# A two-layer diffusion backbone in fp32: the first FFN's down product whole, by seven block products, and the late modulation in three places

## The chip, the core and the metric

The kernel runs on one core of a Trainium2 chip. Its engines run side by side, each through a queue of its own in order: TensorE (PE in the profile, PEld for its weight loads), VectorE (DVE), ScalarE (ACT), GpSimd (POOL) and SyncE (SP), which here only issues DMA transfers. TensorE writes to PSUM, 8 banks of 128 x 512 fp32 values; DVE and ACT carry sums from there to SBUF. The metric is the device time in microseconds, as the median of several runs.

## What is computed

There are 512 latent and 256 context tokens of width 1024, which are 6 tiles of 128 tokens: tiles 0 to 3 latent, 4 and 5 context. Two layers follow each other. Layer 0 has a mixer of gated linear attention and softmax attention, layer 1 a gated recurrence (HGRN2); each is followed by a SwiGLU FFN with 2816 hidden units. Every sub-layer is wrapped in norms and in a modulation that depends on the condition:

```python
m_lat = jnp.split((sc @ mod_w[l] + mod_b[l])[:, None, :], 6, axis=-1)
m_ctx = jnp.split((scc @ mod_w[l] + mod_b[l])[None, None, :], 6, axis=-1)
...
h_lat = _modulate(_rms(x_lat, norm_pre_ffn[l]), m_lat[3], m_lat[4])
x_lat = x_lat + m_lat[5] * _rms(_swiglu(h_lat, ffn_w_gate[l], ffn_w_up[l], ffn_w_down[l]), norm_post_ffn[l])
...
def _swiglu(h, w_gate, w_up, w_down):
    return (jax.nn.silu(h @ w_gate) * (h @ w_up)) @ w_down
```

The context takes the same path with `m_ctx` in layer 0; in layer 1 only latent tokens go through the FFN. So the first FFN has 6 tiles, the second 4. Each `mod_w[l]` is a 1024 x 6144 matrix that is multiplied by two vectors.

## The kernel before

**Precision.** A product in fp32 is made from three matmuls. Each operand is split into a rounded part H (an ACT cast) and a rest L (a DVE subtraction), and `mm3` (line 686) adds H.H, H.L and L.H. So each block of weights costs a DMA of fp32 values into a `raw` tile, a cast on ACT and a subtraction on DVE (`unit`, line 671). The pool `wp` holds three `raw` buffers and four each of `wH` and `wL`.

**Seven products.** `seven` (line 775) multiplies two blocks of 128 hidden columns (a pair) by all tokens by a scheme of the Strassen-Winograd kind. The weights are cut into 2 x 2 blocks, and so are the activations (`Forms`, line 63: halves of the width by halves of the tokens, n = 384 tokens in the first FFN and 256 in the second). Seven products of 4 x 3 matmuls stand for eight. `pair_operands` (line 737) makes the weights' sums and splits on DVE and ACT. Results are put together by DVE and ACT from the banks A, B, D and E; the fourth product (U2) adds onto the bank of the first (A) after that one was copied out.

**First FFN** (`ffn`, line 1510). For each of 11 pairs it runs the gate product, then the part of the down product for the pair before, then the up product. `acc_part` (line 817) is that down part: for each of 6 tiles and two halves of the width 2 blocks by three matmuls of 512 columns, and a DVE addition into `y`. The last call takes two pairs at once and ends one tile after another: `end` runs the post-norm, the residual sum and the next layer's pre-norm on ACT, DVE and POOL (`post_pre`, line 1467), and leaves a function in `turns` that transposes the tile on PE and applies the modulation. `turn(left)` (line 1481) calls these until `left` remain. The values of the second mixer (`odd_values`, line 1308; 512 of 1024 columns) follow in between, with two of their four weight pairs held in tiles of the FFN's own pool. The first pair is special (`first`): its products start while the last tiles of the mixer's output are still being normed, and `turn` is called after 12 and after 36 of its matmuls.

**Second FFN** (`ffn_whole`, line 1613, and `down`, line 1688). All gate and up products come first; the gated activations stay in SBUF (`G`). Then the down product is made whole by seven block products: 2 x 2 blocks over tokens, hidden blocks (even and odd) and output columns. Each of the seven runs over 11 hidden blocks in 7 groups, for the 2 tiles of a token half. `operands` splits weights and activations per group, three groups ahead; sums of weight blocks are made in two SBUF tiles, the first by a DVE addition, later ones by GpSimd transfers that add in memory.

**Modulation.** `mod_vec` (line 515) computes late jobs on DVE: per 128 rows of `mod_w` a load of 0.5 MB and one multiply-add per stream and row block (line 537), then four matmuls that sum over partitions. It is a generator; each step is drawn where the FFN calls `fill`. Five jobs run so in the first FFN. `mod_group` (line 491) is the other way, on PE: 4 matmuls of 256 columns per 128 rows.

**Order.** A planner orders the instructions of each engine when the kernel is built, by their place in the program and by modelled times; where `pinned` is set, PE keeps the written order. In `ffn` it is not set, in `down` and in the second mixer's heads it is.

Of the kernel before, what the change touches and what calls it, by code (L numbers as in the profile page):

```python
# [8 lines left out]
F32 = mybir.dt.float32  # L9
# [8 lines left out]
P = 128  # L18
# [298 lines left out]
class Net:  # L317
# [196 lines left out]

    def mod_vec(self, pool, jobs, own=None, bufs=2, sums=2):
# [259 lines left out]
    def seven(self, W, h, X, fill, then=None, turned=False):  # L775
# [3 lines left out]
        c11, c12, c21, c22 = (X[:, i, n * k : n * k + n] for i in range(2) for k in range(2))  # L779
# [36 lines left out]

    def acc_part(self, parts, n, tiles, groups, ys, first, end):


        nc = self.nc  # L820

        def add(y, pt):
            if first:
                nc.scalar.copy(y, pt)
            else:
                nc.vector.tensor_tensor(y, y, pt, op=ALU.add)  # L826

        for group in groups:
            pts = {}
            for i in group:  # L830

                self.whole = not self.whole
                pt = self.mm_tile("acc") if self.whole else None
                pts[i] = pt, [pt[:, :512], pt[:, 512:]] if self.whole else [self.sc_tile("acc", x) for x in range(2)]
            for p, (units, act) in enumerate(parts):
                done = p == len(parts) - 1
                for i in group:
                    whole, halves = pts[i]
                    t = tiles[i]
                    H, L = (x[:, :, i * P % n : i * P % n + P] for x in act[i * P // n])  # L840
                    for hf in range(2):
                        cs = slice(hf * 512, hf * 512 + 512)
                        for c, unit in enumerate(units):
                            self.mm3(
                                halves[hf],
                                (H[:, c, :], L[:, c, :]),
                                (unit[0][:, 0, cs], unit[1][:, 0, cs]),
                                p == 0 and c == 0,
                                done and c == len(units) - 1,
                            )  # L850
                        if done and hf == 0:
                            self.turn(1)
                        if done and whole is None:
                            add(ys[:, t, cs], halves[hf])
                    if done:
                        if whole is not None:
                            add(ys[:, t, :], whole)
                        end(ys[:, t, :], t)
# [449 lines left out]
    def odd_values(self, fi, h, c0, tiles, us=None):  # L1308

        us = us or self.wide_units(3 * D + c0)  # L1310
        for t0 in tiles:
            pt = self.mm_tile("nat").rearrange("p (a b) -> p a b", a=2)
            for a in range(2):
                self.wide_tile(pt[:, a, :], us, h, t0 + a)
            self.nc.scalar.copy(fi[:, t0 : t0 + 2, c0 : c0 + 512], pt)
# [194 lines left out]
    def ffn(self, l, xp, yp, fp, pp, rp, h, ending, extra=None):  # L1510
# [3 lines left out]
        wg, wu, wd = I["ffn_w_gate"][l], I["ffn_w_up"][l], I["ffn_w_down"][l]  # L1514
        tiles, n = h.order, h.n
        extra = extra(fp) if extra else iter(())
        fill = lambda *_: next(extra, None)
        singles = [(i,) for i in range(len(tiles))]

        gp = rp if l else fp  # L1520
        self.banks(True)

        def gu(x):
            return fp.tile([P, 2, 2 * n], F32, tag=x, bufs=2 if x == "go" else 1, name=x)

        def gated(pool, k, g, u, HL=None, mult=True):

            g, u = (x[:, :, n * k : n * k + n] for x in (g, u))
            if mult:
                nc.vector.tensor_tensor(u, u, g, op=ALU.mult)  # L1530
            H, L = HL or h.gated_tiles(pool, k)
            nc.scalar.copy(H, u)
            nc.vector.tensor_tensor(L, u, H.bitcast(F32), op=ALU.subtract)
            return H, L

        def first():

            cur = h.gated if l else [h.gated_tiles(gp, k) for k in range(2)]
            g, u = gu("go"), gu("uo")
            us = [[self.unit_cols(w, i * P) for w in (wg, wu)] for i in range(2)]  # L1540
            h.open(xp)
            for half in range(2):
                pm = self.mm_tile("pearly")
                pts = [[self.sc_tile("pearly", x)[:, :n] for x in range(2)], [pm[:, 512 * x : 512 * x + n] for x in range(2)]]
                tok = slice(n * half, n * half + n)
                for ks in ((range(4), range(4, 8)) if half == 0 else (range(8),)):
                    for i in range(2):
                        for m in range(2):
                            for k in ks:
                                self.mm3(pts[i][m], tuple(x[:, k, :] for x in us[i][m]), h.raw(k, half), k == 0, k == KD - 1)  # L1550
                            if ks[0] == 0 and half == 0 and m == 0:
                                self.turn(1 - i)
                for i in range(2):
                    nc.scalar.activation(g[:, i, tok], pts[i][0], AF.Silu)
                    nc.vector.tensor_tensor(u[:, i, tok], g[:, i, tok], pts[i][1], op=ALU.mult)
                gated(gp, half, g, u, cur[half], False)
                if half == 0:
                    pp.release()
                    tp = self.open_pool(f"t{l}")
                    h.sums(tp)  # L1560
            h.late()
            return tp, cur

        def units(c0):
            return [self.rows_unit(wd, c0 + i) for i in range(2)]

        def product(w, c0, x, then=None):
            x = gu(x)
            self.seven(self.pair_operands(tp, w, c0 * P, [tp] if l else [], 1 + l), h, x, fill if c0 > 2 else lambda: None, then)
            return x  # L1570

        tp, cur = first()
        y = None
        todo = None
        for c0 in range(2, NFC, 2):
            g = product(wg, c0, "go", todo)
            for k in range(2):
                x = g[:, :, n * k : n * k + n]
                nc.scalar.activation(x, x, AF.Silu)
            if c0 + 2 < NFC:  # L1580
                if y is None:
                    y = yp.tile([P, len(tiles), D], F32, tag="y", bufs=1, name=f"y{l}")
# [4 lines left out]
                def todo(g=g, u=u, cur=cur):  # L1587
                    for k in range(2):
                        gated(gp, k, g, u, cur[k], True)
# [531 lines left out]
```

## Time and profile before

| | us |
|---|---|
| median of 3 runs | 1721.51 (1720.88 to 1721.73) |
| profiled execution | 1719.44 |
| its span, first to last instruction | 1717.5 |
| granted clock of TensorE, mean | 0.997 |

The profile is of one execution. Busy times are per engine. A row of the stretches gives the stretch, then for PE, PEld, DVE, ACT and POOL the busy time and the number of instructions, then the granted PE clock (1.00 is full), the busy share of the DMA engines and GB/s. A row of a group gives line, engine, operation, output <- inputs, shape and count, then busy time and the mean of one instruction in ns, then idle time ahead of it and what ended it. A row of waits gives who waited for whom, the sum in us, how often, and the longest. A row of the chain gives start, length and what ran.

| stretch (us) | what runs |
|---|---|
| 416 to 471 | first FFN: first pair, last tiles of the mixer's output, first pair of `seven` |
| 471 to 909 | pairs: gate, part of down, up |
| 909 to 947 | last down part with the tiles' norms |
| 947 to 1014 | values of the second mixer |
| 1361 to 1592 | second FFN, gate and up |
| 1592 to 1717 | second FFN, down product and ending |

### The profile page before, as it was taken

To read this page: it belongs to the slowest core of one execution; us is meant where nothing else is said; L and a number is where in the kernel's file an instruction comes from. 1 tells how busy PE (TensorE), PEld (TensorE's weight loads), DVE (VectorE), ACT (ScalarE), POOL (GpSimd) and SP (SyncE) were. 2 spreads that over 40 slices of the span, in tenths; PEclk is the share of its full clock that TensorE was granted. 3 is DMA by queue.
4 is the path that set the end of the run, shared out by engine and by line. 5 is a ranking of instruction groups with operands and counts; after the bars stand their busy time and mean duration, and the time that the engine had idled before them with its cause. 6 is when DMAs were issued, how large, how long until landed. Compare 5 with 4: busy or idle time off the path is not lost.

```text
span 1717.5 us, 32485 instructions
## 1 busy us (share of the span) xinstructions
PE 1665.1 (97%) x13446; PEld 1494.9 (87%) x13446; DVE 1301.8 (76%) x2110; ACT 894.8 (52%) x1552; POOL 96.8 (6%) x114
## 2 busy tenths in 40 slices
PE   6999998999999999999999999999999999999997
PEld 5899987887999988999998888988888899999776
DVE  4889678835968999797667418788774599987977
ACT  4745568846453233333346526666564565554554
POOL 1004110000000000000001000000000100000220
PEclk9999999999999999999999999999999999999999
DMA  9641012144334456362224322111124334332883
GB/s 323 191 150 39 2 51 88 49 160 144 102 94 123 151 172 195 109 212 74 74 74 171 106 66 63 51 51 51 50 65 145 123 111 123 100 114 76 224 187 105
DMA packets 177343, 195.87 MB, mean 114 GB/s; under 512 B 6918, under 2 KB 141612, under 8 KB 177196
## 3 DMA queue, kind: packets, MB, share of 16 engines
q1 hardware_dynamic: 170704, 181.56, 33.9%
q0 software_dynamic: 4560, 8.65, 2.8%
q10 hardware_dynamic: 1932, 3.59, 0.6%
q8 instruction: 105, 1.72, 0.4%
q14 instruction: 42, 0.34, 0.1%
HBM read 184.31 MB, written 9.46 MB: 113 GB/s over the span
## 4 chain that ended last, share of the span: by engine, by line
PE 77%; DVE 11%; DMA 5%; ACT 4%; issue 2%; POOL 1%; ACTq 0%; DVEq 0%; POOLq 0%; SPq 0%
PE nat L355 12%; PE a L355 10%; PE acc L355 8%; PE ff L355 8%; PE E L355 7%; PE oproj L355 5%; PE b L355 3%; PE D L355 3%; PE fq L355 3%; PE x L355 2%; PE gqk L355 2%; DMA mraw<-in_mod_w_dram 2%; DVE macc L537 2%; PE o L355 2%; PE S L355 1%
## 5 line engine op out<-in xcount | busy, mean ns | idle before, releaser
L355 PE MATMUL nat<-wH,x 128*128 128x256 f32 (+2 forms) x944 | 215.7, 318 | 3.0 <-ACT x L648 2.6
L734 ACT CAST wH<-raw 128x1024 fp32r<-128x1024 f32 x120 | 125.0, 1051 | 176.6 <-DVE y L826 42.6
L680 DVE TENSOR_TENSOR wL<-raw,wH 128x1024 fp32r<-128x1024 f32 (+1 forms) x104 | 124.1, 1202 | 83.0 <-ACT wH L679 82.2
L355 PEld LDWEIGHTS nat<-wH,x 128*128 128x128 f32 x944 | 157.6, 190 | 18.5 <-ACT x L648 3.6
L735 DVE TENSOR_TENSOR wL<-raw,wH 128x1024 fp32r<-128x1024 f32 x120 | 145.5, 1219 | 34.1 <-ACT wH L734 34.1
L679 ACT CAST wH<-raw 128x1024 fp32r<-128x1024 f32 (+1 forms) x104 | 106.8, 1038 | 80.3 <-PE nat L355 23.7
L355 PE MATMUL nat<-wL,x 128*128 128x256 f32 (+2 forms) x472 | 148.5, 315 | 0.0
L607 POOL TENSOR_TENSOR rs<-ms,neghalf 128x1 f32<-128x1 f32 (+2 forms) x62 | 58.1, 939 | 1277.7 <-DVE ms L605 1277.6
L537 DVE SCALAR_TENSOR_TENSOR macc<-mraw,scT,macc 128x1024 f32<-128x1024 f32 x98 | 122.7, 1277 | 7.3 <-DMA mraw<-in_mod_w_dram 6.9
L355 PE MATMUL ff<-x,wH 128*128 128x512 f32 (+1 forms) x512 | 127.6, 340 | 0.0
L355 PE MATMUL acc<-wH,gH 128*128 128x512 f32 x264 | 104.5, 396 | 1.9 <-DVE y L826 1.3
L355 PE MATMUL acc<-wL,gH 128*128 128x512 f32 x264 | 103.2, 391 | 1.4 <-DVE wL L680 1.4
L355 PE MATMUL acc<-wH,gL 128*128 128x512 f32 x264 | 103.2, 391 | 0.0
L355 PE MATMUL oproj<-wH,x 128*128 128x512 f32 x320 | 101.9, 395 | 0.6 <-ACT x L1241 0.6
L355 PEld LDWEIGHTS ff<-x,wH 128*128 128x128 f32 x512 | 87.3, 190 | 10.1
L355 PEld LDWEIGHTS nat<-wL,x 128*128 128x128 f32 x472 | 89.8, 190 | 5.2
L929 ACT COPY qkh<-arr 128x512 f32<-128x512 f32 x112 | 70.0, 641 | 36.3 <-DVE arr L934 32.1
L355 PE MATMUL ff<-x,wL 128*128 128x256 f32 (+1 forms) x256 | 86.2, 337 | 0.0
L826 DVE TENSOR_TENSOR y<-y,acc 128x512 f32<-128x512 f32 (+1 forms) x81 | 68.9, 861 | 22.6 <-PE acc L355 21.2
L759 DVE TENSOR_TENSOR raw<-raw 128x512 f32<-128x512 f32 x120 | 82.4, 687 | 2.0
L934 DVE TENSOR_TENSOR arr<-arr,f 128x512 f32<-128x512 f32 x112 | 74.1, 686 | 1.9 <-ACT qkh L929 0.3
L355 PE MATMUL a<-T,wH 128*128 128x384 f32 (+1 forms) x320 | 70.4, 309 | 1.7 <-ACT G L797 1.7
(417 smaller groups left out, 4401.4 us busy)
## 6 DMA issues: line engine op xcount, KB each, us to landing
mraw<-in_mod_w_dram SPq DMA_DIRECT2D x80, 512.0 KB, 4.0
raw<-in_ffn_w_gate_dram SPq DMA_DIRECT2D x44, 512.0 KB, 3.9
raw<-in_ffn_w_up_dram SPq DMA_DIRECT2D x44, 512.0 KB, 4.4
raw<-in_odd_w_in_dram SPq DMA_DIRECT2D x40, 512.0 KB, 3.8
raw<-in_ffn_w_down_dram SPq DMA_DIRECT2D x24, 512.0 KB, 3.6
mraw<-in_mod_w_dram SPq DMA_DIRECT2D x32, 256.0 KB, 6.1
raw<-in_even_w_in_dram SPq DMA_DIRECT2D x16, 512.0 KB, 3.9
x<-xr SPq DMA_DIRECT2D x14, 512.0 KB, 2.6
```

The lines of the kernel that those rows point to most:

```text
L355: return self.pin(self.nc.tensor.matmul(*a, **k))
L537: nc.vector.scalar_tensor_tensor(a, u, w, a, op0=ALU.mult, op1=ALU.add)
L607: nc.gpsimd.tensor_tensor(rs, ms, self.neghalf.to_broadcast([P, w]), op=ALU.pow)
L679: nc.scalar.copy(H[:, :m], raw[:, :m])
L680: nc.vector.tensor_tensor(L[:, :m], raw[:, :m], H[:, :m].bitcast(F32), op=ALU.subtract)
L734: self.nc.scalar.copy(H, f)
L735: self.nc.vector.tensor_tensor(L, f, H.bitcast(F32), op=ALU.subtract)
L759: add = lambda o, x, y: nc.vector.tensor_tensor(o, x, y, op=ALU.add)
L826: nc.vector.tensor_tensor(y, y, pt, op=ALU.add)
L929: nc.scalar.copy(qkv[:, :, :, half, :], dst)
L934: nc.vector.tensor_tensor(dst, dst, tb, op=ALU.mult)
```

## The change

- The first FFN uses the scheme of the second: `ffn` now serves both, `acc_part` and `ffn_whole` are gone. Gated activations stay in SBUF, the diagonal ones in a pool of their own (`qa`), the others (`qb`) in tiles that are free at that time. The first FFN has one `go` buffer for the gate product where it had two.
- `down` takes 3 tiles per token half in the first FFN. It adds up the weight blocks in the tiles of the activations' forms (`xp`), which are free when the products end; nothing is loaded early there. Its groups are 1, 2, 2, 2, 2, 1, 1 blocks for both FFNs (before: 1, 1, 2, 2, 2, 2, 1), the token halves change roles, and the last product uses the banks X. In the first FFN tiles 4, 5 and 0 end after the sixth product and are transposed within the last; tiles 1, 2 and 3 end with the last product.
- `turn` in the first pair comes after 36 and 72 matmuls, as in the second FFN.
- The late modulation: the first job by `mod_step` on PE, two jobs by `mod_vec` in the FFN (8 steps drawn per pair, where it was about 10 per longer pair), one beside the first half of the values, one beside the second half.
- The values are made tile by tile. All four weight pairs of the first half are in `wp`.
- The scratch for GpSimd's transfers is 1024 bytes, before 2048.

```diff
+    def mod_step(self, l, m, then=None):
+        self.mod_tiles(l, (m,))
+        acc = self.tr_tile("mod_acc")[:, :256]
+        for k in range(KD):
+            u = self.mod_loads(l, (m,), k, None, 2)[0]
+            yield
+            for j in range(4):
+                self.mm(
...
+        turned = self.mod_cols(l, acc, 256, [(m, r, 0, 0, r, 4) for r in range(2)])
+        yield
+        turned()
...
+    def odd_value(self, fi, h, c0, t, us):
+        pt = self.mm_tile("nat")[:, :512]
+        self.wide_tile(pt, us, h, t)
+        self.nc.scalar.copy(fi[:, t, c0 : c0 + 512], pt)
...
-        self.odd_values(fi, h, 512, (4, 0, 2))
         with self.pool("hg") as gp:
+            us = self.wide_units(3 * D + 512)
+            mods = self.mod_vec(gp, ((1, ((4, 0), (5, 0)), (5, R_NQF, 1)),))
+            for t in (4, 5, 0, 1, 2, 3):
+                self.odd_value(fi, h, 512, t, us)
+                for _ in range(4):
+                    next(mods, None)
+            for _ in mods:
+                pass
...
+        fill = lambda: [next(extra, None) for _ in range(2)]
...
+            step = fill if idx > 1 else lambda: None
+            g = other if l and idx % 2 else go()
...
+            self.seven(self.pair_operands(tp, wu, c0 * P, more(), 1 + l), h, four(idx), step, None, bool(l))
+
+            def todo(g=g, i=idx):
+                g4 = g.rearrange("p a b -> p (a b)").rearrange("p (a b) -> p a b", a=4)
+                nc.vector.tensor_tensor(qa[:, i], qa[:, i], g4[:, 1:3], op=ALU.mult)
+                nc.vector.tensor_tensor(qb[i], qb[i], g4[:, 0:4:3], op=ALU.mult)
                 minus(i)
...
-        groups = [slice(0, 1), slice(1, 2)] + [slice(i, min(i + 2, np_)) for i in range(2, np_, 2)]
+        groups = [slice(0, 1)] + [slice(i, i + 2) for i in range(1, 9, 2)] + [slice(9, 10), slice(10, 11)]
...
+            tb = [xp.tile([P, 6, 512], F32, tag=f"x{x}", bufs=1, name=f"t{x}") for x in range(4)]
...
-        seven = (("11", "X"), ("S1", "O"), ("N3", "Q"), ("SN", "X"), ("S3", "X"), ("22", "O"), ("12", "Q"))
+        seven = (("11", "X"), ("S1", "O"), ("N3", "Q"), ("SN", "X"), ("S3", "X"), ("22", "O"), ("12", "X"))
...
+        out = {"X": [one(f"x{i}") for i in range(nh)], "O": [one(f"o{i}") for i in range(nh)]}
+        out["Q"] = [self.tr_tile("q") for i in range(2)] + out["O"][2:]
...
+                if p == 6 and not l and i == nh - 1 and 3 <= g <= 5:
+                    self.turn(5 - g)
...
                 elif name == "22":
+                    if i == 0:
+                        qp.release()
+                        end, final, follow = ending(dp)
                     plus(y1[:, low], b)
-                    end(y1, tiles[nh + i])
+                    end(y1, t1)
...
         def late_mods(pool):
+            yield from self.mod_step(0, 5, (5, R_NQF))
+            yield from self.mod_vec(pool, ((1, ((0, 0), (0, 1)), None), (1, ((1, 0), (1, 1)), None)))
...
             def values():
+                self.banks(False)
+                fi = yp.tile([P, len(order), D], F32, tag="y", bufs=1, name="fi")
+                us = self.wide_units(3 * D)
+                mods = self.mod_vec(fp, ((1, ((2, 0), (3, 0)), (2, R_NQM, 1)),))
+                for x, t in enumerate(order):
+                    self.turn(max(0, 4 - x))
+                    self.odd_value(fi, h1, 0, t, us)
+                    for _ in range(3):
+                        next(mods, None)
+                for _ in mods:
+                    pass
                 ep.release()
+                return fi
...
-    nc = bacc.Bacc("TRN2", target_bir_lowering=False, num_devices=1, dynamic_dma_scratch_size=2048)
+    nc = bacc.Bacc("TRN2", target_bir_lowering=False, num_devices=1, dynamic_dma_scratch_size=1024)
```

More of the change, by code (lines that the diff above doesn't have):

```diff
@@ L815, in seven @@
                 nc.vector.scalar_tensor_tensor(c22, pt, -1.0, c22, op0=ALU.mult, op1=ALU.subtract)
[L817 to L858, printed above, removed]
     def rows_unit(self, w, c, pool=None):
@@ L1557, in first @@
[L1557 to L1570, printed above, removed]
@@ L1593, in ffn @@
-        for _ in extra:
-            pass
-        tp.release()
-        if gp is not rp:
-            rp.release()
-        self.banks(False)
-        end, follow, pool = ending(y)
-        last = [gated(pool, k, g, u) for k in range(2)]
-        parts = [(units(c0 - 2), cur), (units(c0), last)]
-        next(follow, None)
-        self.acc_part(parts, n, tiles, [(0, 1)] + singles[2:], y, False, end)
-        for left in (2, 1, 0):
-            next(follow, None)
-            self.turn(left)
-        next(follow, None)
```

273 lines of the change are left out of this document (111 added, 162 removed).

## The prediction

> **What bounds the kernel now.** I read the page first: the engines' shares, then the chain that ended last.
>
> ```profile
> span 1717.5 us, 32485 instructions
> PE 1665.1 (97%) x13446; PEld 1494.9 (87%) x13446; DVE 1301.8 (76%) x2110; ACT 894.8 (52%) x1552; POOL 96.8 (6%) x114
> PE 77%; DVE 11%; DMA 5%; ACT 4%; issue 2%; POOL 1%; ACTq 0%; DVEq 0%; POOLq 0%; SPq 0%
> ```
>
> Three quarters of the chain is TensorE, but DVE's 11% says that it comes close in places. The change lies in the first FFN (about 416 to 947 us) and the values behind it, so next I took busy times by stretches there: two pairs of hidden blocks with modulation work, one pair without, three products in a row, the last accumulation with its norms, and the values.
>
> ```profile
> core 0: us, PE busy (x) PEld busy (x) DVE busy (x) ACT busy (x) POOL busy (x), PEclk, DMA share, GB/s
> 516.90:565.00 48.10, 48.10 (x260) 43.89 (x259) 43.66 (x55) 15.02 (x21) 0.00 (x0) 1.00 0.43 129
> 565.00:614.00 49.00, 48.44 (x258) 43.88 (x256) 47.80 (x60) 16.84 (x24) 0.00 (x0) 1.00 0.47 145
> 802.90:849.00 46.10, 46.10 (x247) 43.00 (x246) 30.57 (x44) 16.21 (x23) 0.00 (x0) 1.00 0.24 69
> 865.30:909.00 43.70, 43.70 (x254) 43.70 (x253) 26.39 (x34) 21.64 (x30) 0.00 (x0) 1.00 0.30 91
> 909.00:947.30 38.30, 37.00 (x178) 30.07 (x178) 32.99 (x44) 25.57 (x53) 5.62 (x8) 1.00 0.53 182
> 947.30:1014.50 67.20, 67.20 (x307) 55.79 (x306) 19.59 (x27) 27.60 (x49) 2.77 (x5) 1.00 0.21 66
> ```
>
> PE never rests in them, so a matmul taken away shortens the time directly. DVE is second: 47.80 of 49.00 us while modulation runs, 30.57 of 46.10 without. The waits of PE between 400 and 1010 us give what there is besides matmuls:
>
> ```profile
> PE hT L358 <- DVE xn L624: 4.7, 3, 3.6
> PE acc L355 <- DVE wL L680: 1.4, 1, 1.4
> PE acc L355 <- DVE y L826: 1.3, 1, 1.3
> PE acc L355 <- ACT y L824: 0.5, 1, 0.5
> ```
>
> **The change, part by part.** *Fewer matmuls.* The old down product takes 72 matmuls of 512 columns for each of 11 pairs of hidden blocks (6 tiles, 2 halves, 2 blocks, 3 terms): 792. The new one takes 7 block products of 11 blocks, 3 tiles and 3 terms: 693. The chain of waits has the pitch:
>
> ```profile
> 523.26 0.99 PE mod_acc L355 x8
> ...
> 849.08 16.36 PE acc L355 x72
> ...
> 867.54 2.08 PE E L355 x12
> ```
>
> 16.36 / 72 = 0.2272 us, so 99 matmuls fewer are **-22.5 us**. Gate and up keep their count; 84 matmuls at 2.08 / 12 make 14.56 us a product, 29.1 us a pair.
>
> *Modulation.* The first of five jobs moves from DVE multiply-adds to PE. The same form of job ran once in the attention stage:
>
> ```profile
> L355 PE MATMUL mod_acc<-mraw,scT x64: 379/379/403, 293.8 to 297.1; 128*32 128x256 f32 x64
> ```
>
> That is 297.1 - 293.8 + 0.4 = 3.7 us of PE, in place of 0.99 us (the x8 row above) and two transposes more: **+2.4 us** (2 to 4, should its eight pieces cost something at each switch). The two jobs that go behind the FFN meet DVE at 19.59 of 67.20 us; one job is some 15 us of DVE by the rows above ((43.66 + 47.80) / 2 - 30.57), and each has six values tiles of 24 matmuls (6 x 24 x 0.2272 = 33 us) beside it. By themselves they cost nothing there (what they do to the norms is counted with the values below); were that cover gone, 15 us each. Their sums' matmuls are only moved.
>
> *Earlier stalls that go.* The first products of the FFN now transpose the last two tiles after 36 and 72 matmuls and not after 12 and 36. The 3.6 us wait above stood at the second place (423.4 us), and the clock fell behind it:
>
> ```profile
> 423.40:427.10 3.70, 0.07 (x2) 0.07 (x2) 3.26 (x7) 3.70 (x10) 0.92 (x1) 1.00 0.85 307
> 427.10:431.00 3.90, 3.90 (x16) 3.68 (x17) 2.45 (x4) 3.87 (x11) 0.00 (x0) 0.56 0.63 236
> ```
>
> It cost 3.6 + 0.44 x 3.9 = 5.3 us. 36 matmuls at 0.173 us are 6.2 us more time, over the 3.6 that lacked. What is late next is the split of those tiles for the second half; the second FFN has these places already, and its waits hold this row, 1.1 us:
>
> ```profile
> PE pearly L355 <- DVE x L98: 1.1, 1, 1.1
> ```
>
> I take **-4.0** (-5.3 to -1). The Trainium skill, "TensorE: Matmul & The Clock Gate", section "What's actually happening", says that an idle window of about 3.4 us halves the clock until about as much work has passed. These two rows agree; by that rule each new gap of such a length would cost an estimated 1.7 us beyond itself. With three such gaps among the new stalls the sum below would by that rule be some 5 us smaller; the row of the second FFN's last product below (0.89) is the only one there with a lowered clock.
>
> The waits of acc (1.4 + 1.3 + 0.5) and the other two of hT (4.7 - 3.6) belong to code that goes: **-4.3** (-2 if their causes return elsewhere, which the next part counts).
>
> *New stalls, first phase.* Three products in a row cost DVE 26.39 / 3 = 8.8 us each at full PE speed, so a pair is 17.6 plus two gating products and a subtraction:
>
> ```profile
> L735 DVE TENSOR_TENSOR wL<-raw,wH 128x1024 fp32r<-128x1024 f32 x55 | 66.7, 1220 | 29.3 <-ACT wH L734 29.3
> L1530 DVE TENSOR_TENSOR uo<-uo,go 128x768 f32<-128x768 f32 x20 | 18.2, 948 | 0.0
> L814 DVE TENSOR_TENSOR go<-go,a 128x384 f32<-128x384 f32 x9 | 4.9, 546 | 0.1
> ```
>
> 17.6 + 2 x 0.95 + 0.55 = 20.0 of 29.1 us. The two DVE jobs left have 10 steps each and 8 are drawn per pair, 2.5 pairs in all: 50 + 30 = 80 us of DVE against 2.5 x 29.1 + 2 = 75. That overload of 5 us (9 by the dearer of the two rows) can be worked ahead in earlier pairs with 9 us free each. **+2** (0 to 9).
>
> *New stalls, down product.* The second FFN already runs this scheme with two tiles for three; its seven products, of which I show those that lost time, and its first phase:
>
> ```profile
> 1592.40:1611.30 18.90, 15.80 (x68) 12.28 (x68) 17.24 (x27) 8.24 (x15) 0.28 (x1) 1.00 0.90 317
> 1626.40:1644.50 18.10, 16.37 (x68) 12.10 (x67) 13.23 (x22) 10.83 (x19) 6.16 (x6) 1.00 1.09 251
> 1659.60:1675.50 15.90, 15.14 (x67) 12.56 (x68) 13.42 (x22) 9.14 (x15) 1.23 (x2) 1.00 0.45 81
> 1690.50:1706.50 16.00, 13.68 (x54) 10.39 (x53) 13.67 (x19) 8.70 (x15) 1.96 (x2) 0.89 0.47 164
> 1425.17:1592.41 167.24, 167.24 (x1392) 167.09 (x1392) 141.35 (x218) 92.21 (x151) 0.00 (x0) 1.00 0.35 100
> ```
>
> The last row shows PE full with DVE at 85%, so the first phase can stand that load. The first: the start lost 18.9 - 66 x 0.2272 = 3.9 us, mostly here:
>
> ```profile
> PE x L355 <- DVE aL L1743: 3.1, 2, 2.4
> PE q L355 <- DVE aL L1743: 2.3, 2, 1.9
> ```
>
> The same start comes in the first FFN: the second block column can be loaded only when the activations' forms are free, 12 matmuls (2.1 us) before the phase ends, and the DVE addition that waits for it stands ahead of the next split. Nothing of the weights is loaded early there, so the first product moves 22 blocks of 0.26 MB in 99 x 0.2272 = 22.5 us, 256 GB/s, under the 317 that the row shows. **+4** (1 to 7). The middle products have 4.1 us of PE for what had 2.7; the losses there (3.1 and 0.9 us) came at DMA shares of 1.09 and 0.45: **+1** (0 to 4). Halving the scratch for GpSimd's transfers lets fewer be under way; the slowest took 13.3 us to land, and two products (45 us) lie before their use:
>
> ```profile
> tc<-in_ffn_w_down_dram POOLq DMA_DIRECT2D x4, 512.0 KB, 13.3
> ```
>
> Nothing, with 0.5 either way for the second FFN's new grouping.
>
> *New stalls, last product and first values.* Tiles 4, 5, 0 end together before the last product, tiles 1, 2, 3 at its end; before, tiles ended one by one. One tile costs:
>
> ```profile
> L638 ACT ACTIVATE hf<-hT,modcol,aff 128x128 f32<-128x128 f32 x48 | 18.6, 468 | 2.1 <-PE hT L358 1.7 <-DVE x L649 0.4
> L649 DVE TENSOR_TENSOR x<-hf,x 128x512 fp32r<-128x512 f32 x12 | 8.3, 688 | 12.2 <-ACT x L648 12.1
> L666 DVE SCALAR_TENSOR_TENSOR xr<-pn,rs,xr 128x1024 f32<-128x1024 f32 x6 | 7.7, 1283 | 2.2 <-POOL rs L607 2.0
> L648 ACT CAST x<-hf 128x512 fp32r<-128x512 f32 x12 | 7.5, 627 | 0.1
> L659 DVE TENSOR_TENSOR pn<-y,gv 128x1024 f32<-128x1024 f32 x6 | 7.3, 1220 | 0.1
> L615 ACT ACTIVATE junk<-y 128x1024 bf16<-128x1024 f32 x6 | 6.4, 1059 | 4.1 <-DVE y L826 4.1
> L624 DVE TENSOR_SCALAR xn<-xr,rs 128x1024 f32<-128x1024 f32 x6 | 4.5, 756 | 3.4 <-POOL rs L607 3.4
> ```
>
> ACT: 8 x 0.39 + 2 x 0.63 + 2 x 1.06 = 6.5 us; DVE: 1.2 + 1.3 + 0.75 + 2 x 0.69 and an addition of 0.7 = 5.3. The last product's operands are 5.5 full groups with a split of 1.22 and one of 0.95 each, 12 us of DVE, and I take the same for ACT's casts. With three tiles that is 31 us of ACT and 28 of DVE beside 22.5 us of matmuls and three tiles' transposes, in a written order, with the three transposes only 4 and 2 us apart where one tile's ACT work takes 4.4. **+4** (1 to 9). The first values tile needs the last four splits and its banks emptied behind three more tiles' norms: **+3** (1 to 7). Three values tiles, 16 us, then hide what is left of those norms. DVE has in the 67 us of both sets of values three norms (16), eight splits (10) and the two jobs (30), 56 us or 84%, and the second set takes the weight buffers that the first holds to its end (before, two pairs were elsewhere): **+2** (0 to 8).
>
> **Sum.** The new stalls are 2 + 4 + 1 + 4 + 3 + 2 = 16. -22.5 + 2.4 - 4.0 - 4.3 + 16 = -12.4. The profiled execution took 1719.44 us for its span of 1717.5; 1707.0 after. The median of the runs, 1721.51, lies 2.1 above it: 1709.
>
> **Rivals.** *The modulation jobs do not run ahead:* the pairs with them are DVE-bound, 9 us in place of 2: 1716. For it, the 47.80 of 49.00; against it, that such pairs now lose only 1 to 2 us.
>
> *The ending eats the gain:* the stalls of the last product and of both sets of values lie at their upper ends (9 + 7 + 8 = 24 in place of 9): 1724, hardly another time than before. For it, the second FFN's last product, PE busy 13.68 of 16.00 us at a clock of 0.89; against it, matmuls of three values tiles as cover, and DVE at 84% there.
>
> *One gate buffer, slower:* the first FFN has two now and is left with one. The first copy of a gate product must wait until the pair before is gated: last two sums 1.1, two gatings 1.9, copy 0.5, some 0.3 of signals = 3.8 us, and the fourth product, 6.2 us in, adds onto that bank. Slack 2.4 us, two splits of 1.22. With work of b us ahead of the gating on DVE, each of nine gate products waits b - 2.4; from b = 4 (9 x 1.6 = 14) the gain is gone, and b = 5.5 (two modulation steps of 2.5 and a wait) gives 28: 1737. Against it: 9 us of DVE are free in each pair.
>
> *Stalls mostly filled* (4 in place of 16): 1697; for it, only 8 us of waits in 600 us now.
>
> **How the numbers follow.** Forecast 0.50, jobs 0.13, ending 0.15, one buffer 0.13, filled 0.09. Faster by over 0.2% (3.4 us, about what a measurement can tell from no change): nearly all of forecast and jobs, a quarter of the ending, all of filled, 0.73; within it 0.11, mostly the ending; slower 0.16, the single buffer and some of the ending. The range runs from the filled case, 1696, to the ending's, 1725, and leaves the single buffer and a few per cent outside.
>
> **What would show it.** A pitch still at 0.227 us over 693 matmuls; no wait of 3.6 us near 423; no ACT copy of a gate product holding the fourth product; down from first to last matmul in 163 to 172 us (693 x 0.2272 = 157.5 of matmuls); values starting within 4 us of its end; the second FFN as long as before. It would be wrong if pairs took over 32 us, or if PE rested more than 20 us between the start of the FFN and the first head.

## The result, and the profile after

| | before | after |
|---|---|---|
| median in the same runs | 1721.62 (1720.88 to 1723.80, 4 runs) | 1773.12 (1768.36 to 1776.52, 4 runs) |
| profiled execution, span | 1719.44, 1717.5 | 1768.36, 1766.6 |

The kernel after takes 1.0295 times the time of before (95% interval 1.0269 to 1.0321): it is slower by some 51 us, where 1709 was forecast. The head of its page and the line of the chain by engine:

```profile
span 1766.6 us, 32663 instructions
PE 1669.6 (95%) x13401; PEld 1488.6 (84%) x13401; DVE 1298.4 (73%) x2121; ACT 928.9 (53%) x1615; POOL 122.6 (7%) x135
PE 69%; DVE 11%; DMA 8%; issue 5%; ACT 5%; POOL 2%; SPq 0%; DVEq 0%; POOLq 0%; ACTq 0%
```

DVE has not more to do than before. The shares that grew in the chain are DMA (5 to 8%), issue (2 to 5%), ACT (4 to 5%) and POOL (1 to 2%). So transfers have come into the path, and that is the first hint of what the prediction left out. The stretches of the kernel after, cut where PE takes up the next stage (columns as before; the first phase of the first FFN is in four pieces):

```profile
core 0: us, PE busy (x) PEld busy (x) DVE busy (x) ACT busy (x) POOL busy (x), PEclk, DMA share, GB/s
452.40:541.00 88.60, 88.60 (x547) 84.65 (x546) 61.11 (x83) 35.80 (x52) 0.00 (x0) 1.00 0.43 131
541.00:582.00 41.00, 37.18 (x205) 33.59 (x204) 37.14 (x46) 12.77 (x19) 0.00 (x0) 1.00 0.52 155
582.00:620.00 38.00, 31.33 (x167) 28.59 (x166) 35.55 (x46) 13.56 (x20) 0.00 (x0) 0.96 0.38 111
620.00:768.60 148.60, 148.60 (x859) 148.60 (x858) 98.88 (x134) 65.89 (x94) 0.00 (x0) 1.00 0.25 71
768.60:943.10 174.50, 163.71 (x719) 133.12 (x717) 127.75 (x165) 92.35 (x145) 29.32 (x27) 0.99 0.61 147
943.10:1021.80 78.70, 72.97 (x325) 56.72 (x326) 47.30 (x56) 34.28 (x66) 4.62 (x7) 1.00 0.65 206
1021.80:1063.50 41.70, 30.31 (x159) 23.43 (x158) 33.08 (x45) 14.59 (x19) 0.00 (x0) 0.85 0.72 226
1063.50:1390.90 327.40, 323.11 (x3473) 280.15 (x3471) 231.22 (x476) 189.90 (x324) 13.79 (x14) 0.99 0.23 70
1417.60:1620.10 202.50, 202.23 (x1683) 201.69 (x1681) 174.72 (x266) 111.99 (x183) 0.00 (x0) 1.00 0.38 111
1620.10:1766.60 146.50, 117.03 (x463) 92.52 (x462) 103.48 (x153) 67.20 (x111) 26.03 (x25) 0.89 0.64 153
```

PE stands most in five places: around 541 to 620, in the first FFN's down product (768 to 943, where the prediction had a loss too), in the values, ahead of the heads, and in the second FFN's down product. Set against the kernel before, by the first matmul of each stage on PE's timeline (the last two columns are runs that are told below, the last by its quickest execution; a head's preparation goes from its forget product, `ff`, to its transposed key, `kcT`):

| stage (us) | before | after | three edits | jobs spread |
|---|---|---|---|---|
| first FFN, first products | 40.6 | 35.1 | 35.1 | 35.1 |
| first FFN, pairs and down product | 490.5 | 490.7 | 477.8 | 479.1 |
| both sets of values | 67.1 | 78.7 | 78.5 | 70.1 |
| first forget product to first transposed key | 25.0 | 41.7 | 25.0 | 26.4 |
| heads, gates, output projection | 321.9 | 327.5 | 331.1 | 329.7 |
| second FFN, first products | 27.5 | 26.7 | 26.7 | 27.3 |
| second FFN, pairs | 203.7 | 202.5 | 202.7 | 202.4 |
| second FFN, down product and ending | 125.1 | 146.5 | 126.2 | 125.5 |

The first FFN as a whole is where the matmuls were saved, and it gives 5 us, all of it in its first products. Then 11.6 are lost in the values, 16.7 ahead of the heads, 5.6 up to the second FFN and 21.4 in the second FFN's down product, in a stage whose matmuls the change did not make fewer or more. PE's waits in three stretches of the kernel after (452 to 769, 1021 to 1064, 1590 to the end):

```profile
PE a L355 <- DVE wL L759: 5.8, 3, 3.4
PE mod_acc L355 <- DVE macc L561: 2.2, 1, 2.2
PE E L355 <- ACT wH L758: 1.6, 1, 1.6
...
PE mod_acc L355 <- DVE macc L561: 9.8, 2, 7.8
...
PE x L355 <- ACT aH L1660: 5.4, 1, 5.4
PE x L355 <- DVE wL L1661: 5.1, 1, 5.1
PE o L355 <- ACT aH L1660: 4.4, 2, 3.0
```

From here came four theories: the small ring, as the scratch for GpSimd's transfers is called from here on (R), bursts of modulation steps (B), the late job's loads (L), and the job and weights beside the first values (V).

### The profile page after: what moved, and what is told of

Read it like the earlier page. It is cut to its first block, busy times and chain, and to the rows that moved or that the text cites. A ratio compares the mean times of both kernels' runs of the same rounds, so it can differ in the third digit from the quotient of the medians.

```text
span 1766.6 us, 32663 instructions
## 1 busy us (share of the span) xinstructions
PE 1669.6 (95%) x13401; PEld 1488.6 (84%) x13401; DVE 1298.4 (73%) x2121; ACT 928.9 (53%) x1615; POOL 122.6 (7%) x135
## 4 chain that ended last, share of the span: by engine, by line
PE 69%; DVE 11%; DMA 8%; issue 5%; ACT 5%; POOL 2%; SPq 0%; DVEq 0%; POOLq 0%; ACTq 0%
PE a L355 10%; PE nat L355 8%; PE ff L355 7%; PE E L355 6%; PE x L355 5%; PE oproj L355 5%; DMA mraw<-in_mod_w_dram 5%; PE o L355 3%; PE b L355 3%; PE D L355 3%; PE pearly L355 2%; DVE macc L561 2%; PE fq L355 2%; PE gqk L355 2%; PE S L355 1%
## 5 line engine op out<-in xcount | busy, mean ns | idle before, releaser
L355 PE MATMUL nat<-wH,x 128*128 128x256 f32 (+2 forms) x992 | 231.0, 323 | 4.9 <-ACT x L672 2.6
L355 PE MATMUL nat<-wL,x 128*128 128x256 f32 (+2 forms) x496 | 158.6, 320 | 3.1 <-DVE wL L704 3.1
L704 DVE TENSOR_TENSOR wL<-raw,wH 128x1024 fp32r<-128x1024 f32 (+1 forms) x84 | 100.0, 1199 | 39.3 <-ACT wH L703 38.5
L703 ACT CAST wH<-raw 128x1024 fp32r<-128x1024 f32 (+1 forms) x84 | 86.1, 1037 | 74.7 <-PE ff L355 16.9
L561 DVE SCALAR_TENSOR_TENSOR macc<-mraw,scT,macc 128x1024 f32<-128x1024 f32 x84 | 105.3, 1280 | 26.5 <-DMA mraw<-in_mod_w_dram 26.3
L355 PE MATMUL x<-wH,aL 128*128 128x512 f32 x220 | 89.4, 407 | 9.1 <-DVE aL L1662 9.1
L1629 POOL DMA_DIRECT2D t<-in_ffn_w_down_dram x42 | 45.4, 1179 | 741.0 <-DVE wL L1661 623.8
L355 PE MATMUL x<-wH,aH 128*128 128x512 f32 x220 | 89.5, 407 | 7.1 <-ACT aH L1660 5.4
L910 ACT COPY qkh<-arr 128x512 f32<-128x512 f32 x112 | 70.1, 642 | 49.1 <-DVE arr L915 35.0
L355 PE MATMUL x<-wL,aH 128*128 128x512 f32 x220 | 89.0, 404 | 5.5 <-DVE wL L1661 5.5
L355 PE MATMUL E<-T,wH 128*128 128x384 f32 (+1 forms) x320 | 70.5, 309 | 1.6 <-ACT wH L758 1.6
```

Of the source, the lines that this page charges most:

```text
L355: return self.pin(self.nc.tensor.matmul(*a, **k))
L561: nc.vector.scalar_tensor_tensor(a, u, w, a, op0=ALU.mult, op1=ALU.add)
L703: nc.scalar.copy(H[:, :m], raw[:, :m])
L704: nc.vector.tensor_tensor(L[:, :m], raw[:, :m], H[:, :m].bitcast(F32), op=ALU.subtract)
L910: nc.scalar.copy(qkv[:, :, :, half, :], dst)
L1629: add = lambda o, src: self.pin(nc.gpsimd.dma_start(out=o, in_=src, accum_op=ALU.add))
```

## The experiments

Times are medians, each with the kernel before run on the same chip.

### The ring alone: on the kernel before, and taken back on the kernel after

```diff
# e1, on before
-dynamic_dma_scratch_size=2048
+dynamic_dma_scratch_size=1024
# e2, on after
-dynamic_dma_scratch_size=1024
+dynamic_dma_scratch_size=2048
```

> The kernel before with its descriptor ring halved from 2048 to 1024 bytes a partition, and nothing else changed. Theory R (the small ring lets one accumulating half-megabyte transfer be under way at a time, and that is what lengthens the second FFN's down product): the down product of the second FFN, about 126 us before, grows by some 15 to 22 us and the whole time to 1735 to 1745 us; the issues of the accumulating transfers come about 4.9 us apart and never two in flight. Rival (the regrouping, the new pools and the spare buffers of the second down product do it, the ring costs nothing): within 2 us of 1721.6 us.

> The kernel after with its ring back at 2048 bytes, every instruction and its order as after. Theory R: the second FFN's down product falls from about 147 us to 125 to 130 us, the first FFN's from 174.5 to 170 to 174 us (its additions are due later, so less hangs on them), the whole time from 1773 to 1748 to 1755 us. Rival (regrouping, pools): 1770 us or more, with the down product of the second FFN still at 145 us or above.

The kernel before with the small ring: 1736.97 us, ratio 1.0091 (1.0076 to 1.0106), 15.3 us slower. The kernel after with the old ring: 1753.14 us, 20.0 us faster than after. The down product of the second FFN took 141.4 us in the first (125.1 before) and 127.0 in the second (146.5 after); no other stage moved by more than 4 us. Theory R holds on both kernels, and the rival falls: all the regrouping of `down` together costs the second FFN 2 us. Two details came out otherwise than expected: the issues stand 6.1 us apart and not 4.9, and the first FFN's down product stayed at 174.1 us instead of falling a little.

The mechanism is seen on POOL's own timeline (start, length, what; in brackets the idle time ahead of it and what ended it). First the kernel after:

```profile
1672.37 1.22 POOL L1629 DMA_DIRECT2D t<-in_ffn_w_down_dram  x1 [5.51 <-DMA raw<-in_ffn_w_down_dram]
1678.58 1.21 POOL L1629 DMA_DIRECT2D t<-in_ffn_w_down_dram  x1 [4.99 <-issue]
1684.70 1.21 POOL L1629 DMA_DIRECT2D t<-in_ffn_w_down_dram  x1 [4.91 <-issue]
```

Then the kernel after with the old ring:

```profile
1643.87 1.22 POOL L1629 DMA_DIRECT2D t<-in_ffn_w_down_dram  x1 [2.48 <-DVE wL L1661]
1646.18 1.20 POOL L1629 DMA_DIRECT2D t<-in_ffn_w_down_dram  x1 [1.09 <-DVE wL L1661]
1648.55 1.21 POOL L1629 DMA_DIRECT2D t<-in_ffn_w_down_dram  x1 [1.17 <-DVE wL L1661]
```

With the small ring the issues stand 6.1 us apart, and POOL waits 4.9 us for nothing that the profile names ("issue"). With the old one they follow each other in 2.3 to 2.4 us, as fast as the operands release them. The landing times say the same: issue rows of the second down product after, then with the old ring (line, engine, count, size, median us from issue to landing):

```profile
t<-in_ffn_w_down_dram POOLq DMA_DIRECT2D x12, 512.0 KB, 5.8
```

```profile
t<-in_ffn_w_down_dram POOLq DMA_DIRECT2D x12, 512.0 KB, 9.1
```

After, a transfer lands sooner (5.8 us against 9.1), and the next one of its size is issued only then: by the trace those issued at 1672.37, 1678.58 and 1684.70 land at 1678.27, 1684.36 and 1690.53, and each time the next issue follows 0.3 us later. One transfer of 0.524 MB in 6.15 us is 85 GB/s. What waits for them is ACT, in the second down product of the kernel after:

```profile
ACT wH L1659 <- DMA t<-in_ffn_w_down_dram: 20.1, 6, 5.0
```

With the old ring no such row is left. That its 20.1 us are so near to the 20.0 us measured is chance, for ACT's waits are not PE's. PE's own rows name casts of activations (`aH`): those are queued on ACT behind the cast that waits for the sum of weights. In that stage PE waited 21.0 us after and 8.6 us with the old ring, 12.4 less. The other 7.1 us of the stage's 19.5 are the clock, granted at 0.89 after and at 0.96 with the old ring, where the same 463 matmuls are busy for 109.89 us instead of 117.03:

```profile
1624.10:1751.10 127.00, 109.89 (x463) 88.31 (x462) 103.13 (x153) 66.88 (x111) 25.85 (x25) 0.96 0.69 176
```

The first FFN pays nothing for the same ring (its down product took 174.5 and 174.1 us).

### How much ring is needed

```diff
-dynamic_dma_scratch_size=1024
+dynamic_dma_scratch_size=1536
```

> The kernel after with a ring of 1536 bytes, nothing else changed. If the ring is filled byte for byte, half of the loss comes back: about 1763 us, with the accumulating transfers overlapping in part. If only whole transfers of half a megabyte count (one in 1024 bytes, two in 2048), 1536 holds one of them and the time is that of 1024, 1768 to 1773 us, with their issues still 6.1 us apart. If 1024 bytes was just short of two, 1536 gives all back: 1750 to 1756 us.

1750.31 us (1749.13 to 1753.44): all of it came back, the third of the three outcomes. Its issues stand 2.4 to 3.7 us apart and land after 7.3 us, so some two are under way at a time:

```profile
1643.21 1.24 POOL L1629 DMA_DIRECT2D t<-in_ffn_w_down_dram  x1 [2.40 <-DVE wL L1661]
1645.57 1.21 POOL L1629 DMA_DIRECT2D t<-in_ffn_w_down_dram  x1 [1.12 <-DVE wL L1661]
1649.29 1.19 POOL L1629 DMA_DIRECT2D t<-in_ffn_w_down_dram  x1 [2.52 <-DVE qa L1667]
```

So what was lost is the second transfer in flight. What more 2048 bytes allow is worth nothing here.

### The late job beside the second values

```diff
 for t in (4, 5, 0, 1, 2, 3):
     self.odd_value(fi, h, 512, t, us)
-    for _ in range(4):
-        next(mods, None)
-for _ in mods:
-    pass
+    next(mods, None)
...
     go(outs, old)
+    go(mods)
     go(new, new)
     go(outs, old, scan)
+    go(mods)
     go(new, new)
...
+for _ in mods:
+    pass
```

This and the next run have the ring at 2048 bytes and are compared with that run.

> As the run with the ring at 2048 bytes, and in the odd mixer the late modulation job of layer 1 (scale and gate of the second FFN, 16 single loads) takes one step behind each of the six value tiles and then two steps a head instead of four steps a tile with all the rest drawn ahead of the first head. Theory L (the job with two load buffers runs at the pace of its loads, about 3.3 us a step, and TensorE stands for its last sum): the stretch from the first forget product to the first transposed key falls from 41.6 us to about 26 us, the whole time by 13 to 17 us. Rival (VectorE work itself binds the second mixer, so the steps only move): the heads grow by as much, and the whole time falls by less than 4 us.

1740.49 us, 12.7 less. The stretch to the first transposed key fell from 42.5 to 25.0 us, the heads grew by 2.4. Theory L holds, with a gain a little under its 13 to 17 us; the rival's 4 us bound is far off. How a job of 16 multiply-adds of at most 1.28 us (20 us of DVE) could take 48 us (1010 to 1058) is seen on the queue of SP in the kernel after:

```profile
995.82 25.27 SPq L461 DMA_DIRECT2D mraw<-in_mod_w_dram  x8
1021.91 0.38 SPq L702 DMA_DIRECT2D raw<-in_odd_w_in_dram  x1
```

and by what DVE waited for there (1000 to 1062) and the page's row of issues:

```profile
DVE macc L561 <- DMA mraw<-in_mod_w_dram: 11.9, 12, 2.3
DVE macc L559 <- DMA mraw<-in_mod_w_dram: 6.0, 2, 3.5
```

```profile
mraw<-in_mod_w_dram SPq DMA_DIRECT2D x80, 512.0 KB, 4.1
```

The first row merges eight loads; its first two still belong to the job before. The job's own 16 steps take 48 us, 3.0 us each (3.3 was expected). There are two buffers, so a load can be issued only when the multiply-add before the last has read its own: on DVE multiply-adds end at 1020.74 and 1023.28 us, on SP loads start at 1020.77 and 1023.30. A load lands 4.1 us after its issue, and 4.1 + 1.28 with two buffers gives an estimated 2.7 us a step at best. DVE stood 18 us for loads. The second row of SP shows weights for the heads behind these loads in its order; no wait of PE in this stretch was for them. Whether more buffers would do as well was not tried.

The stall also shows the clock. Six stretches of the kernel after, from the last long wait on:

```profile
1044.00:1049.00 5.00, 2.95 (x25) 2.74 (x23) 4.78 (x7) 1.44 (x2) 0.00 (x0) 1.00 0.82 245
1049.00:1053.00 4.00, 0.00 (x0) 0.00 (x0) 3.59 (x6) 0.00 (x0) 0.00 (x0) 0.70 0.69 232
1053.00:1057.00 4.00, 1.92 (x4) 0.19 (x4) 3.61 (x6) 1.59 (x3) 0.00 (x0) 0.50 0.76 247
1057.00:1063.50 6.50, 3.25 (x10) 1.15 (x11) 5.08 (x12) 2.29 (x4) 0.00 (x0) 0.50 0.00 0
1063.50:1067.00 3.50, 3.04 (x10) 2.25 (x9) 2.90 (x7) 1.78 (x4) 0.00 (x0) 0.50 0.01 1
1067.00:1071.00 4.00, 4.00 (x17) 3.24 (x17) 0.14 (x1) 0.00 (x0) 0.00 (x0) 0.92 0.01 4
```

PE rested 7.8 us, and the granted clock fell to 0.50. It stayed there while four short pieces with waits of up to 2.0 us between them followed, and came back only within the last row, after some 4 us of nearly full work. The Trainium skill, "TensorE: Matmul & The Clock Gate", section "What's actually happening", says that the clock halves after an idle window of about 3.4 us and returns after about as long a busy one. These rows agree, the value of 0.50 too.

### One modulation step a fill

```diff
-fill = lambda: [next(extra, None) for _ in range(2)]
+fill = lambda: next(extra, None)
```

> As the run with the ring at 2048 bytes, and in the first FFN's gate and up products each fill draws one modulation step instead of two; the steps spread over seven pairs instead of four. Theory B (bursts of four multiply-adds stand ahead of the weight splits on VectorE, and TensorE waits for those): the first phase falls from 316 us to 300 to 306 us, the whole time by 10 to 16 us. Rival (VectorE has too much to do in all, or the loads are late): the rests only spread, the phase stays within 4 us of 316 us.

1738.33 us, 14.8 less than the run with the ring alone. The first phase took 301.7 us (316.1). Theory B holds. What had stood in the way, on DVE's timeline of the kernel after:

```profile
541.98 5.06 DVE L561 SCALAR_TENSOR_TENSOR macc<-mraw,scT,macc 128x1024 f32<-128x1024 f32 x4 [0.81 <-DMA mraw<-in_mod_w_dram]
...
557.98 4.86 DVE L561 SCALAR_TENSOR_TENSOR macc<-mraw,scT,macc 128x1024 f32<-128x1024 f32 x4
...
564.58 0.69 DVE L469 COPY modrows<-mod_acc 128x512 f32<-128x512 f32 x1 [1.27 <-PE mod_acc L355]
```

Four multiply-adds are 5 us in one piece, in front of splits of weights that PE needs every few us. DVE's own waits from 541 to 620 are smaller: 2.5 us for these loads and 1.3 for a sum of PE. The same stretches with one step a fill:

```profile
542.00:583.00 41.00, 41.00 (x244) 40.22 (x241) 31.98 (x45) 16.08 (x24) 0.00 (x0) 1.00 0.39 121
583.00:621.00 38.00, 37.97 (x219) 37.66 (x219) 37.90 (x48) 16.43 (x23) 0.00 (x0) 1.00 0.42 125
```

In the second stretch DVE is busy for 37.90 of 38.00 us, more than in that stretch of the kernel after (35.55), and PE does not wait. So it was the order, not the sum of the work. The edit both cuts the bursts and spreads the steps over more pairs, and this run does not tell the two apart.

### The three together

> The three edits together: ring at 2048 bytes, one modulation step a fill, the late job drawn two steps a head. If the three causes are independent their gains add: 1773.1 less 20.0, 14.8 and 12.7 is 1725.6 us, and 1722 to 1730 is expected. Rival (they share a stall, so that one gives back what another saves): above 1733 us.

1723.93 us (1722.00 to 1725.59, 10 runs), ratio 1.0013 (1.0003 to 1.0024). The gains add, as expected (1725.6), so the three causes are independent to 2 us. Without them the new scheme is still not faster than the kernel before. What remains is in the table above: the first FFN gives 12.7 + 5.5 us, and 11.4 go in the values and 9.2 in the heads.

### What remains: the job beside the first values, and the banks

```diff
# e6, on the three edits: both single jobs in the heads
-mods = self.mod_vec(fp, ((1, ((2, 0), (3, 0)), (2, R_NQM, 1)),))
...
-mods = self.mod_vec(gp, ((1, ((4, 0), (5, 0)), (5, R_NQF, 1)),))
+mods = self.mod_vec(gp, ((1, ((2, 0), (3, 0)), (2, R_NQM, 1)), (1, ((4, 0), (5, 0)), (5, R_NQF, 1))))
...
+    go(mods)
...
# e7, on the three edits
 us = self.wide_units(3 * D)
+pt = self.mm_tile("nat")
...
-    self.odd_value(fi, h1, 0, t, us)
+    self.odd_value(fi, h1, 0, t, us, None if x else pt)
# e9, on the three edits
 us = self.wide_units(3 * D)
+for i in range(2):
+    self.sc_tile("lay", i)
```

> As the run with the three edits, and the other single-stream job (gate of the second mixer and shift of the second FFN) is taken out of the stage of the first values too: both jobs are drawn five steps a head behind the second values. Theory V (the job's loads and its two sums on TensorE are what makes the first values late): the stage of the values falls from about 80 us to 70 to 74 us, the heads grow by 2 to 4 us (two column sums of 1.05 us and the turns move there), and the whole time is 1717 to 1722 us. Rival (the turns of the last four tiles and the second set's weights make it late by themselves, or VectorE becomes the bound in the heads): the stage stays at 77 us or more, or the heads grow by what it loses; the whole time within 3 us of the run with the three edits.

1723.86 us, no gain (ratio to before 1.0011, 0.9996 to 1.0025). Both theories were half right. The values fell to 72.6 us as V said; but the stretch to the first key grew by 5.7 and the heads by 2.9, as the rival said. Rows of that run, the values, that stretch and the heads:

```profile
930.90:1003.50 72.60, 70.12 (x313) 57.73 (x313) 38.87 (x44) 35.42 (x67) 4.31 (x7) 0.98 0.55 179
1003.50:1034.20 30.70, 27.96 (x145) 24.70 (x144) 15.72 (x21) 10.70 (x13) 0.00 (x0) 0.89 0.46 137
1034.20:1368.20 334.00, 325.55 (x3501) 280.72 (x3500) 254.22 (x511) 192.80 (x330) 13.70 (x14) 1.00 0.30 94
```

> As the run with the three edits, with one edit that moves no work: the first value's PSUM tile is taken ahead of the first turn, so that the banks are laid out as in the kernel before (wide tiles first, not the transposes). Theory P (the 3.4 us in front of the second FFN's first products is a bank that is released late because the layout changed): the wait in front of the first gate product of the second FFN falls from 3.4 to about 0.5 us, the whole time by 2 to 3 us. Rival (the wait is for the gate rows or the weights): it stays, and the whole time with it.

> As the run with the three edits, with another layout of the PSUM banks and no work moved: the two half-width tiles are taken ahead of the first turn, so that the wide tiles of the odd mixer's output projection come to lie in the last banks, away from those that the second FFN's first products take. Theory P2 (the 3.36 us ahead of those products is the wait for the last projected tile's bank to be read by its norm; taking a wide tile first left the wide tiles in the first banks): the wait goes to below 0.5 us and the whole time falls by 3 us, to about 1721 us. Rival (the wait is for something that no bank order changes): 3.36 us again, and 1723 to 1725 us.

With the wide tile taken first: 1724.52 us, ratio 1.0021 (1.0007 to 1.0035), and the wait ahead of the second FFN is still there:

```profile
PE pearly L355 <- DVE ms L629: 3.4, 1, 3.4
```

So P falls as it was put. With the half-width tiles taken first, no wait of PE is left in that place (1330 to 1370 us), and the stage of the heads is 2.6 us shorter than with the three edits; 1722.19 us (12 runs), ratio 1.0004 (0.9992 to 1.0015). The whole time alone does not tell this run from the three edits, for the intervals overlap; the stage and the missing wait do. So it is a bank, as P2 said: which tile is taken first decides whether the second FFN's first products wait. Why the kernel before waits only 0.5 us there, and why taking a wide tile first does not bring that back, is not shown.

```diff
# e10, on e9 and e6: two steps beside a tile of the second values, then four a head from the second head on
-    next(mods, None)
+    go(mods, mods)
...
+late = mods if hd else iter(())
...
+go(late)
```

> As the run before it in this call, and both single-stream jobs taken out of the stage of the first values, drawn two steps beside each tile of the second values and four steps a head from the second head on, none in the first. Theory V2 (their loads and sums cost TensorE only where they meet the first values' weights or the first head's preparation): the stage of the values 72 to 74 us as in the run without a job there, the stretch to the first transposed key back at 25 us against 30.7, the whole time 1713 to 1718 us. Rival (VectorE in the heads has no more room, 39 of 40 us busy in the first head with one job): the heads grow by what the values lose, 1720 to 1724 us.

1720.99 us (1714.13 to 1724.10, 12 runs), ratio 1.0000 (0.9988 to 1.0012). By the stages of its profiled execution V2 holds: values 70.1 us, then 26.4 to the first key, and the heads, with both jobs, 329.7 against 328.5 in the run before it:

```profile
930.80:1000.90 70.10, 68.65 (x312) 56.55 (x313) 38.97 (x44) 34.67 (x67) 4.31 (x7) 1.00 0.57 185
1000.90:1027.30 26.40, 25.25 (x145) 22.17 (x144) 14.84 (x21) 10.71 (x13) 0.00 (x0) 1.00 0.50 149
```

But that is its quickest execution (1714.13). The median lies in the rival's span and only 1.2 us below the run before it, which the intervals do not tell apart. So the whole time that V2 forecast was not reached. It has the lowest median of the new scheme's versions, level with the kernel before.

## Why the prediction was wrong

The saving of matmuls came as forecast. What failed are stalls that the sum had at nothing or at a few us: the ring (0, measured 20.0), the modulation steps in the first phase (2, measured 14.6), the job beside the second values (0, measured 12.7).

**The ring** was the largest miss. "Nothing, with 0.5 either way" was worked out from the time that one transfer takes to land (13.3 us) against two products until its use. That is a latency; what halving took away was throughput. Three products in a row (S1, N3, SN) send 33 blocks of 0.262 MB, 8.65 MB; at 85 GB/s that is 102 us. The last of these sums is used in the product 22, the fifth from S1 on. In the first FFN five products last 5 x 22.5 = 112 us, which is enough, and nothing was lost there. In the second a product is 66 x 0.2272 = 15 us, and five are 75. There the issues went from 1636.9 to 1725.3 us after, 88 us, and from 1640.5 to 1690.8 with the old ring, 50 us. The 45 us in the text belonged to the first FFN, while the row with 13.3 us was of the second. The fill itself was in the rows of before (two issues of the second FFN's down product, and a row of landings); 8.5 to 13.3 us to land with issues 2 to 4 us apart mean several in flight:

```profile
1616.41 1.19 POOL L1707 DMA_DIRECT2D tb<-in_ffn_w_down_dram  x1 [1.13 <-DVE wL L1742]
1618.82 1.20 POOL L1707 DMA_DIRECT2D tb<-in_ffn_w_down_dram  x1 [1.22 <-DVE wL L1742]
```

```profile
tb<-in_ffn_w_down_dram POOLq DMA_DIRECT2D x8, 512.0 KB, 8.5
```

**First phase, "+2 (0 to 9)":** it cost 14.6 (316.3 less 301.7). With one step a fill the same work costs no wait, so the sum of DVE work was not at fault. The step that failed is "can be worked ahead in earlier pairs": the steps are drawn where the code draws them, two at a time, and a row of four multiply-adds delays the next split by 5 us however much room the pair has on average. The rival with the jobs that do not run ahead had the place, at 9 us.

**The moved jobs, "By themselves they cost nothing":** the job beside the second values cost 12.7 us. Its DVE time was counted and covered; its 16 loads through two buffers were not: the step listed none of the DMAs that it moved. The job beside the first values lengthened that stage by 5.9 to 8.4 us (78.5, without it 72.6 and 70.1); the term there, "+2 (0 to 8)", was at its upper end. Drawn five steps a head from the first head on, the job cost 5.7 + 2.9 us behind the values for the 5.9 it gave there. Drawn two steps a value tile and then from the second head on, it cost 1.4 us up to the first key and 1.3 in the heads, by the profiled executions.

**A term that was missing:** 3.4 us ahead of the second FFN, for the banks. The lower clock behind new stalls stood in the prediction as an aside outside the sum; it is 7.1 of the ring's 20 us.

**Down product, 163 to 172 us:** 174.5, 17 above its matmuls. By PE's timeline the start took 3.2 (+4 in the sum), the five middle products 2.1 (+1), and the last product, up to the first matmul of the values, 11.8 (+4, 1 to 9), in it 2.2 us of wait for a transposition behind ACT's work. So the places were right and the last product was sized too small. The start of the values, within 4 us, held.

**What held.** The saving of 99 matmuls: one middle product is 99 matmuls in 22.6 us, 0.228 each. The turns: first products 35.1 for 40.6 us, 5.5 less (4.0 taken, 5.3 at most), and no wait of 3.6 us. Of this 2.1 us may be one execution's: in the profile of the kernel before with the small ring the same products took 38.5 us, with a wait of 3.2 us and no fall of the clock. The job on PE: 64 matmuls in 5.1 us in the run with one step a fill, where 3.7 was taken; 2.4 becomes 3.8, within the 4 allowed for its switches. No gate copy holds a fourth product, and with one step a fill the first phase has no wait at all, so the single `go` buffer costs nothing. The mark "PE rested more than 20 us between the start of the FFN and the first head" was passed: 38 us by the table of stretches.

**What stays open:** how many bytes of ring one transfer takes. By the landing times in the traces, with a transfer of 256 KB counted as half of one of 512 KB, at most 1.5 are under way with 1024 bytes, 2.5 with 1536 and 3.5 with 2048. On that count one of 512 KB takes over 512 and at most 585 bytes. Why the median of the spread version is 7 us above its profiled execution is settled in part: the mean granted clock was 0.995 in that execution, 0.993 in the next quickest (1716.22 us) and 0.988 to 0.991 in the other ten. Why the clock differs between executions of one kernel is open.

## What to carry to other kernels

Before shrinking a buffer that holds transfers in flight, count from the rows before how many are in flight (landing time over distance of issues) and what the stream needs per stage; the time until use says nothing of it. Work that is hidden by the sum of busy times still has to be cut to pieces shorter than the slack of what it stands in front of. A job that is moved takes its loads along: with two buffers it goes at best at the pace of half of landing plus use.

## What the runs showed of the hardware

Of the accumulating transfers of 512 KB that GpSimd issues, only one at a time is on its way with a ring of 1024 bytes (issues 6.1 us apart, 85 GB/s), while with 1536 and 2048 bytes the first of them follow each other within 2.3 to 3.7 us. With the small ring GpSimd stands 4.9 us ahead of an issue, and the profile names no releaser. The Trainium skill, "DMA: Bandwidth & Descriptors", section "SWDGE vs HWDGE vs iDMA", says that GpSimd writes the descriptors of such transfers into rings that lie in a part of SBUF; these runs agree with that in so far as the size set aside decides when the next can be issued.
